# Weight units one unit later in the load queue, and the sample stage laid out anew, in a two-layer hybrid decoder step

## The chip, the cores and the metric

The kernel runs on one core of a Trainium2 chip, as one launch. The metric is the device time of an execution in microseconds. Before the change it is 2910.22 us, the median of three runs (2906.68 to 2913.82). The profile is that of one further execution, which took 2911.25 us; its span, from the first to the last instruction, is 2909.6 us.

## The reference

One inference step of two layers for a prompt of 256 tokens and for a sample group of 8 sequences of 8 new tokens behind 1024 past ones: 320 token columns, which share all weights. Model width 2048, MLP width 8192, all in f32.

```
layer 0   z = rmsnorm(x) @ w_in                   # rx rg | q kc vc ks vs kw vw | gates
          A) rx -> causal conv (4) -> RG-LRU scan;  y_rnn = gelu(rg) * h       (1024 channels)
          B) sparse attention, 16 query heads, 4 kv heads of 64, three branches:
             compressed  blocks of 64 tokens -> k, v by a small MLP (w1, gelu, w2)
             selected    prompt: all its blocks; sample: 16 blocks, chosen by the compressed probabilities
             window      the last 512 tokens
             o = sum of branches * sigmoid gates
          x += concat(y_rnn, o) @ w_out ;  x += relu(rmsnorm(x) @ ff1)^2 @ ff2
layer 1   x += gated short convolution (w_in, w_out) ;  x += the same MLP
```

A sample reads its past keys and values through a page table: 8 pages of 128 rows for the compressed branch, 8 for the selected one, and 512 window rows. The outputs also hold the new keys, values, windows and recurrent states.

## The kernel before

**Weights.** Every large product runs in `gemm` (L173). A weight unit is 512 KB; `w_dma` (L133) loads it on SP's queue into one of four buffers (`NRAW`). ScalarE and VectorE split it into two numbers of the matmul type, a high part `whi` (`S.copy`, L145) and the rest `wlo` (L146), in six half units (`NSP`). Each weight tile then gives three matmuls of 320 columns (L204 to L206), 24 in a unit. `w_fill` (L149) runs before each half unit: it issues the conversions up to three units ahead of the matmuls, and then the loads:

```
while st["dma"] < min(st["conv"] // 2 + NRAW, len(units)):
    w_dma()
```

**Slots.** After each unit `side()` counts a slot and issues what `at(n, f)` has put there, in the order of the calls. All other work of layer 0 is hung into slots in this way. Each engine takes its instructions in program order; so a wait holds all that stands behind it on the same engine. DMAs issued by `SP` and `G` stand in the order of those queues too. Slots 1 to 42 are the projections of keys, values, queries and gates, 43 to 74 those of rx and rg, in eight groups of four slots (`C0 = 42`); then comes the first half of the output projection, 16 units.

**Compression** (slots 5 to 46). `cmp_load` brings eight pages of a sequence on SP (eight register reads of page numbers, then eight DMAs, tile `cx`), `cmp_swap` (L703) turns them into `cy` by two copies on VectorE, one on POOL, one on ScalarE, and `cmp_mm` (L713) multiplies by `w1`, which `cmp_load_w` (L679) has loaded on SP. Right behind the matmuls the two halves of their sum are emptied, for 16 pages in two rounds of a copy on ScalarE (L719) and an add on VectorE (L720) into `hid`, a part of `yr`.

**Prompt stage** (slots 45 to 63, `P3 = 45`). `pr_slot` (`pr_scores`, `pr_softmax`, `pr_scale`, `pr_trans`, `pr_pv`) takes one head pair and branch per slot. The recurrence of rx runs beside it: per pair of channel chunks `rec_conv`, `rec_gates`, three steps of `rec_scan` (the scan itself is L616, in `rec_scan_c`), `rg_gelu_a`, `rg_gelu_b` and `rec_y` (L625, POOL). For the last pair these are slots 70 to 76.

**Sample stage** (from slot 65, `P4 = 65`, three slots per sequence). `sa_open` (L1182, slot 63) opens its buffers in memory that the prompt stage has left, loads the first keys and hangs in the sixteen copies that lay out the queries (`sa_q`, L1201, POOL) and the first value loads (`sa_load_v`, L1160, on POOL's queue, with eight register reads per sequence). `sa_begin` (slot 64) makes the first keys' scores: queries by compressed keys and by the new keys, the first softmax; `sa_select` (slot 66) chooses the blocks. Per sequence b: `sa_kt` in slots n, n and n+1 turns the three key tiles `kl` (L1168) and then loads the next sequence's on SP (L1153); `sa_scores` (L1264) and `sa_softmax` (L1288 to L1296) in n+2; `sa_trans` (L1307) in n+4; `sa_pv` (L1325 to L1330) in n+5, which at its end issues the value loads of the next sequence; `sa_ot` (L1341) in n+7. PSUM has three banks for `gemm`, four `a` for all small work and one `o`.

**Between the stages.** After the last rg unit two `side()` run without weight matmuls, the memory of the recurrence and of `yh`, `yl` is given back, `xh`, `xl` and `y` are made there, `y` is loaded from DRAM on ScalarE's queue (L1422), eight chunks of `yr` are split (L445, L446), a third `side()` runs, and the output projection begins; `half_evac` (L1432) adds its sums to `y`.

Of the kernel before, what the change touches and what calls it, by code (L numbers as in the profile page):

```python
# [11 lines left out]
F32 = mybir.dt.float32  # L12
# [58 lines left out]
def tile_hybrid_step(ctx: ExitStack, tc: tile.TileContext, A, O, stop=None, dbg=None):  # L71
# [181 lines left out]
    kc_x = kb.tile([128, 4, 8], F32, name="kc_x")  # L253
    vc_p = kb.tile([64, 8, 2, 64], F32, name="vc_p")
    kt = {b: kb.tile([128, 2, N], F32, name="kt_" + b) for b in ("s", "w")}
    kx = {b: kb.tile([128, 2, NP_TOK], F32, name="kx_" + b) for b in ("s", "w")}
    vp = {b: kb.tile([128, 2, 256], F32, name="vp_" + b) for b in ("s", "w")}
    gp = kb.tile([128, 2, 48], F32, name="gp")
    tbc = kb.tile([128, 2, 4, 16], F32, name="tbc")
# [446 lines left out]
    def cmp_mm(bp, i, pages):  # L706

        y = cx.pop(("y", bp, i)).rearrange("p d h s n -> p d (h s n)")
        p = bank("a")
        n = pages * 8  # L710
        for d in range(16):
            for u in range(2):
                PE.matmul(p[64 * u:64 * u + 64, :n], w1[:, i, 16 * u + d], y[:, 16 * u + d],  # L713
                          start=d == 0, stop=d == 15)
        nh = min(pages, 8)
        for k in range(pages // nh):
            h = hid[64 * i:64 * i + 64, 16 * bp + 8 * k:16 * bp + 8 * k + nh].rearrange("p n g s -> p s (n g)")
            q = p[:, 64 * k:64 * k + 8 * nh].rearrange("p (s n) -> p s n", s=2)
            S.copy(h, q[64 - 64 * i:128 - 64 * i])  # L719
            V.tensor_tensor(h, q[64 * i:64 * i + 64], h, ALU.add)  # L720
# [281 lines left out]

    p3x = ctx.enter_context(ExitStack())
    p3 = tb = pct_p = None

    def p3_open():
        nonlocal p3, tb, pct_p
        cmpx.close()
        ev.close()
        p3 = p3x.enter_context(pool("p3", "right"))  # L1010
# [125 lines left out]
    p4 = ld = None  # L1136
# [9 lines left out]
    def sa_load_k(b, c):  # L1146
        k = ld.tile([128, 4, 256], F32, name="kl", bufs=3)
# [27 lines left out]
    def sa_open():  # L1175
        nonlocal ld, p4, pc, pcT, snew, mnew, badd, wtab, ot_s, qx
        ld = p4x.enter_context(pool("ld", "right"))
        p4 = p4x.enter_context(pool("p4", "right"))
        pc = p4.tile([128, NB, 16], F32, name="pc")
        pcT = p4.tile([128, 128], F32, name="pcT")  # L1180
        snew = p4.tile([128, 2, NB, NT], F32, name="snew")
        mnew = p4.tile([128, 2, NB], F32, name="mnew")  # L1182
        badd = p4.tile([128, NB, 16], F32, name="badd")
        wtab = p4.tile([128, 512], F32, name="wtab")
        ot_s = p4.tile([128, 8, NB * NT], F32, name="ot_s")
# [19 lines left out]
    def sa_begin():  # L1205
        V.tensor_copy(wtab[:, :384], near[:, 0:1].to_broadcast([128, 384]))
# [22 lines left out]
        mx = p4.tile([128, NB], F32, name="mx")  # L1229
# [7 lines left out]
    def sa_select():  # L1237
        mx = p4.tile([128, NB], F32, name="mx")
# [6 lines left out]
        im = p4.tile([128, NB, 14], F32, name="im")  # L1245
# [21 lines left out]
    def sa_softmax(b):  # L1267
# [26 lines left out]
        V.tensor_tensor(l[:, 0:2], l[:, 0:2], l[:, 2:4], ALU.add)  # L1294
        V.reciprocal(l[:, 0:2], l[:, 0:2])
        V.tensor_tensor(l[:, 0:2], l[:, 0:2], gs[:, 1:3, b], ALU.mult)  # L1296
        sj["p", b] = (s, l)

    def sa_trans(b):
        s, l = sj["p", b]  # L1300
        t = p4.tile([128, 14, 128], F32, name="pT")
        sj["pt", b] = t
        for i in range(4):
            p = bank("a")
            n = min(4, 13 - 4 * i)
# [29 lines left out]
    def sa_ot(b):  # L1335
        r = sj.pop(("o", b))
        o = bank("a")
# [31 lines left out]
    def p3_close():  # L1369
        p3x.close()  # L1370
        kbx.close()
# [17 lines left out]
    P4 = P3 + 20  # L1389
    at(P4 - 1, sa_begin)  # L1390
    at(P4 + 1, sa_select)
# [19 lines left out]
    for _ in range(2):  # L1411
        side()
    rgp.close()
    base.close()
    actp = ctx.enter_context(ExitStack())
    act = actp.enter_context(pool("act"))

    xh = act.tile([128, 16, N], F32R, name="xh")
    xl = act.tile([128, 16, N], F32R, name="xl")
# [14 lines left out]
    run(gemm(8, 8, lambda k: (xh[:, k], xl[:, k]), half_evac, 256))  # L1434
# [10 lines left out]
    p4x.close()  # L1445
    l0.close()
# [245 lines left out]
```

## Time and profile before

| of the profiled execution | |
|---|---|
| time / span | 2911.25 / 2909.6 us |
| TensorE (PE) busy | 2846.3 us, 98% |
| VectorE (DVE) busy | 1618.6 us, 56% |
| ScalarE (ACT) busy | 1213.1 us, 42% |
| GpSimd (POOL) busy | 378.2 us, 13% |
| moved by DMA | 463.98 MB, 159 GB/s as a mean |
| mean granted TensorE clock | 0.990 |

The page gives the busy time of each engine; the answers of the trace give waits (who waited for whom), windows (busy time, granted clock and DMA share in a stretch), instructions of a line, and a timeline. In a timeline a row is start, duration, engine, line, operation, what it writes and reads, how many were merged, and in brackets the idle time of the engine before it with what ended it. The DMA share is the mean busy share of the core's 16 DMA engines.

### The profile page before, as it was taken

The page shows a single profiled execution, that of the slowest core. Times are in us where ns is not written, and L with a number is a line of the kernel's source. Part 1 is how long each engine was busy: PE and PEld are TensorE (multiplying, and loading weights), DVE is VectorE, ACT ScalarE, POOL GpSimd, SP SyncE. Part 2 cuts the span into 40 slices and gives each one's busy share as a digit, 9 for nine tenths or more (in the row PEclk, how much of TensorE's full clock was granted, in tenths as well). Part 3 has the DMA queues.
Part 4 walks back from the last instruction along what each step waited for, and adds up shares of the span by engine and source line. Part 5 has one row for each costly group of instructions (what it writes and reads, how often), then busy time and mean ns, then how long its engine had stood idle before and what let it go on. Part 6 is the DMA issues. An engine that isn't in the chain of part 4 may idle for free.

```text
span 2909.6 us, 53661 instructions
## 1 busy us (share of the span) xinstructions
PE 2846.3 (98%) x20947; PEld 2785.6 (96%) x20947; DVE 1618.6 (56%) x2937; ACT 1213.1 (42%) x2336; POOL 378.2 (13%) x555
## 2 busy tenths in 40 slices
PE   8999987999999999999999999999999999999999
PEld 7998776899999999999999999999999999999999
DVE  6796677774444544544465555555444444544544
ACT  4555644354334434434443333344433433433433
POOL 2323353230010010010010111111011011001000
PEclk9999989999999999999999999999999999999999
DMA  8765258645445555555445444444444444544543
GB/s 244 213 198 156 73 147 257 210 138 162 165 154 167 165 159 161 165 166 153 153 144 156 152 147 150 147 153 148 149 152 145 153 152 149 149 152 148 149 157 119
DMA packets 275997, 463.98 MB, mean 159 GB/s; under 512 B 19050, under 2 KB 100694, under 8 KB 275215
## 3 DMA queue, kind: packets, MB, share of 16 engines
q1 hardware_dynamic: 268254, 438.47, 49.1%
q0 software_dynamic: 6864, 19.44, 2.1%
q8 instruction: 164, 2.69, 0.4%
q10 hardware_dynamic: 624, 2.64, 0.2%
q14 instruction: 91, 0.74, 0.1%
HBM read 452.95 MB, written 15.92 MB: 161 GB/s over the span
## 4 chain that ended last, share of the span: by engine, by line
PE 81%; DVE 0%; DMA 0%; ACT 0%; issue 0%; DVEq 0%; ACTq 0%
PE ps_g L204 27%; PE ps_g L206 27%; PE ps_g L205 27%; DMA wraw<-in_w_out_e_dram 0%; PE ps_a L1652 0%; DVE wlo L146 0%; PE ps_a L1264 0%; PE ps_o L1325 0%; PE ps_a L1307 0%; DVE ktl L1168 0%; PE ps_a L633 0%; PE ps_a L1624 0%; DVE rs L1473 0%; PE ps_a L436 0%; DVE y L1475 0%
## 5 line engine op out<-in xcount | busy, mean ns | idle before, releaser
L146 DVE TENSOR_TENSOR wlo<-wraw,whi 128x512 fp32r<-128x512 f32 x1488 | 1007.4, 718 | 1122.3 <-ACT whi L145 1121.5
L145 ACT CAST whi<-wraw 128x512 fp32r<-128x512 f32 x1492 | 854.1, 617 | 1377.8 <-PE ps_g L206 1334.0
L204 PE MATMUL ps_g<-yl,whi 128*128 128x320 f32 x3408 | 1066.9, 313 | 10.9 <-DVE kv L817 5.1
L205 PE MATMUL ps_g<-yh,wlo 128*128 128x320 f32 x3408 | 1056.8, 310 | 0.0
L206 PE MATMUL ps_g<-yh,whi 128*128 128x320 f32 x3408 | 1056.6, 310 | 0.0
L204 PE MATMUL ps_g<-xl,whi 128*128 128x320 f32 x2560 | 796.2, 311 | 11.3 <-DVE xl L446 7.3
L206 PE MATMUL ps_g<-xh,whi 128*128 128x320 f32 x2560 | 792.7, 310 | 0.0
L205 PE MATMUL ps_g<-xh,wlo 128*128 128x320 f32 x2560 | 792.7, 310 | 0.0
L204 PEld LDWEIGHTS ps_g<-yl,whi 128*128 128x128 f32 x3408 | 643.2, 189 | 22.3 <-issue 8.4
L205 PEld LDWEIGHTS ps_g<-yh,wlo 128*128 128x128 f32 x3408 | 643.3, 189 | 1.7 <-issue 0.2
L206 PEld LDWEIGHTS ps_g<-yh,whi 128*128 128x128 f32 x3408 | 643.2, 189 | 0.0
L204 PEld LDWEIGHTS ps_g<-xl,whi 128*128 128x128 f32 x2560 | 482.4, 188 | 13.1 <-DVE xl L446 7.7
L205 PEld LDWEIGHTS ps_g<-xh,wlo 128*128 128x128 f32 x2560 | 482.4, 188 | 0.0
L206 PEld LDWEIGHTS ps_g<-xh,whi 128*128 128x128 f32 x2560 | 482.1, 188 | 0.0
L1477 POOL TENSOR_TENSOR y<-y,rs 128x320 f32<-128x320 f32 x96 | 92.3, 994 | 1257.8 <-DVE rs L1473 1257.8
L1473 DVE TENSOR_TENSOR rs<-ps_g,r 128x320 f32<-128x320 f32 x128 | 60.6, 488 | 25.1 <-PE ps_g L206 25.0
L1506 DVE TENSOR_TENSOR fr<-fr 128x320 f32<-128x320 f32 x128 | 62.3, 487 | 11.1 <-ACT xh L1509 11.1
L431 POOL TENSOR_TENSOR nacc<-nacc,nsq 128x320 f32<-128x320 f32 x45 | 44.1, 980 | 172.0 <-ACT nsq L427 170.4
L1507 DVE TENSOR_TENSOR xl<-fr,xh 128x320 fp32r<-128x320 f32 x128 | 62.9, 492 | 4.4
L1509 ACT ACTIVATE xh<-fr 128x320 fp32r<-128x320 f32 x128 | 60.3, 471 | 4.1
L1503 ACT ACTIVATE fr<-ps_g 128x320 f32<-128x320 f32 x128 | 56.1, 438 | 5.7 <-PE ps_g L206 5.7
L1586 POOL TENSOR_TENSOR xx<-cg,r 128x256 f32<-128x256 f32 x16 | 13.1, 819 | 278.4 <-DVE xx L1584 278.4
(382 smaller groups left out, 1426.3 us busy)
## 6 DMA issues: line engine op xcount, KB each, us to landing
wraw<-in_w_ff_dram SPq DMA_DIRECT2D x512, 512.0 KB, 3.7
wraw<-in_w_in_o_dram SPq DMA_DIRECT2D x96, 512.0 KB, 3.7
wraw<-in_w_in_e_dram SPq DMA_DIRECT2D x74, 512.0 KB, 5.3
wraw<-in_w_out_e_dram SPq DMA_DIRECT2D x32, 512.0 KB, 5.5
wraw<-in_w_out_o_dram SPq DMA_DIRECT2D x32, 512.0 KB, 3.9
cx<-in_cache_cmp_k_dram SPq DMA_DIRECT2D x64, 128.0 KB, 2.1
cx<-in_cache_cmp_v_dram SPq DMA_DIRECT2D x64, 128.0 KB, 3.4
kl<-in_cache_sel_k_dram SPq DMA_DIRECT2D x64, 128.0 KB, 3.6
```

What stands on the lines that cost most here:

```text
L145: S.copy(h, r)
L146: (G if u < 4 and hf == 0 else V).tensor_tensor(l, r, h.bitcast(F32), ALU.subtract)
L204: PE.matmul(ps[m][:, :N], wh, al, start=k + j == 0, stop=False)
L205: PE.matmul(ps[m][:, :N], wl, ah, start=False, stop=False)
L206: PE.matmul(ps[m][:, :N], wh, ah, start=False, stop=k + j == nk - 1)
L431: G.tensor_tensor(nacc["t"], nacc["t"], sq, ALU.add)
L1473: V.tensor_tensor(t, ps[:, :N], scale, ALU.mult)
L1477: after(1, lambda: G.tensor_tensor(y[:, c], y[:, c], t, ALU.add))
L1503: S.activation(t, ps[:, :N], AF.Relu)
L1506: V.tensor_tensor(t, t, t, ALU.mult)
L1507: V.tensor_tensor(xl[:, c], t, xh[:, c].bitcast(F32), ALU.subtract)
L1509: after(1, lambda: S.activation(xh[:, c], t, AF.Square))
```

## The change

- Weight loads: `w_fill` keeps one unit less issued ahead of the conversions, so a unit stands one place later in SP's queue. The buffers are the same four.
- `cmp_load_w` issues its loads on POOL (`G`).
- The compression sum is emptied by `cmp_evac`, hung into the next slot (the last one at once), with one copy and one add for all pages.
- The prompt's keys, values and gates (pool `keep_b`) become views of one tile `kba`; in the sample stage the value tiles and `ot_s` lie in it.
- A new pool `ldk`, opened with the prompt stage, holds the key tiles and the small tables. `sa_begin` moves to slot 50, `sa_select` to 52, the first key loads to 55, 56 and 57; `P4` is 64. The first value loads move one slot forward, to between the query copies; four of the sixteen query copies go to ScalarE.
- The scaling factors `l` move from `sa_softmax` to `sa_trans`. `sa_ot` takes bank `o`.
- The first half of the output projection uses `yh`, `yl` as `xh`, `xl`: six chunks are split right after the last rg unit, the first projection unit runs, then one `side()` without weight matmuls, the `y` loads and the split of the last two chunks.

```diff
-        while st["dma"] < min(st["conv"] // 2 + NRAW, len(units)):
+        while st["dma"] < min(st["conv"] // 2 + NRAW - 1, len(units)):
...
+    kba = kb.tile([128, 4608], F32, name="kba")
...
-            SP.dma_start(w1[64 * hf:64 * hf + 64, i], A["cmp_w1_" + nm_][0][:, 32 * hf:32 * hf + 32])
-        SP.dma_start(w2[64 * i:64 * i + 64, 64 * i:64 * i + 64], A["cmp_w2_" + nm_][0])
+            G.dma_start(w1[64 * hf:64 * hf + 64, i], A["cmp_w1_" + nm_][0][:, 32 * hf:32 * hf + 32])
+        G.dma_start(w2[64 * i:64 * i + 64, 64 * i:64 * i + 64], A["cmp_w2_" + nm_][0])
...
+        if (bp, i) == (3, 1):
+            cmp_evac(bp, i, pages, p)
+        else:
+            at(st["slot"] + 1, cmp_evac, bp, i, pages, p)
+
+    def cmp_evac(bp, i, pages, p):
         nh = min(pages, 8)
-        for k in range(pages // nh):
...
+        h = hid[64 * i:64 * i + 64, 16 * bp:16 * bp + pages].rearrange("p (k n) g s -> p k s (n g)", n=nh)
+        q = p[:, :8 * pages].rearrange("p (k s n) -> p k s n", k=pages // nh, s=2)
+        S.copy(h, q[64 - 64 * i:128 - 64 * i])
+        V.tensor_tensor(h, q[64 * i:64 * i + 64], h, ALU.add)
...
-        v = ld.tile([128, 4, 256], F32, name="vl", bufs=4)
+        o = 1024 * ((3 * b + c) % 4)
+        v = kba[:, o:o + 1024].rearrange("p (n c) -> p n c", n=4)
...
-        for c in range(3):
-            sa_load_k(0, c)
...
-            at(n + 2, sa_load_v, 0, c)
-        at(n + 4, sa_load_v, 1, 0)
+            at(n + 1, sa_load_v, 0, c)
+        at(n + 3, sa_load_v, 1, 0)
...
-                G.tensor_copy(
+                (G.tensor_copy if gg or half else S.copy)(
...
-        o = bank("a")
+        o = bank("o")
...
-    P4 = P3 + 20
-    at(P4 - 1, sa_begin)
-    at(P4 + 1, sa_select)
+    P4 = P3 + 19
+    at(P3 + 5, sa_begin)
+    at(P3 + 7, sa_select)
+    for c in range(3):
+        at(P3 + 10 + c, sa_load_k, 0, c)
...
-    for _ in range(2):
-        side()
+
+    xh, xl = yh, yl
+    for c in range(0, 6, 2):
+        split(xh[:, c:c + 2], xl[:, c:c + 2], yr[:, c:c + 2])
+    half = gemm(8, 8, lambda k: (xh[:, k], xl[:, k]), lambda g, m, ps: half_evac(g, m, ps), 256)
+    next(half)
+    side()
     rgp.close()
-    base.close()
...
     for c in range(4):
         S.dma_start(y[:, 4 * c:4 * c + 4], xt_d[:, 4 * c:4 * c + 4])
-    for c in range(0, 8, 2):
-        split(xh[:, c:c + 2], xl[:, c:c + 2], yr[:, c:c + 2])
-    side()
+    split(xh[:, 6:8], xl[:, 6:8], yr[:, 6:8])
...
-    run(gemm(8, 8, lambda k: (xh[:, k], xl[:, k]), half_evac, 256))
+    run(half)
```

## Rows read from the trace of the kernel before

**Rows 1.** Windows: stretch, busy us of each engine (instructions), clock, DMA share, GB/s.

```profile
600.00:2905.00 2305.00, 2304.43 (x15724) 2302.37 (x15722) 1172.27 (x1966) 908.80 (x1695) 180.08 (x243) 1.00 0.49 153
```

**Rows 2.** Waits of TensorE, 60 to 240 us: total us, times, longest us.

```profile
PE ps_g L204 <- DVE kv L817: 5.1, 2, 4.2
PE ps_a L713 <- DMA w<-in_cmp_w_k_dram: 4.1, 1, 4.1
PE ps_g L204 <- DVE qr L882: 4.0, 2, 2.9
PE ps_a L713 <- DVE yr L703: 2.5, 1, 2.5
```

**Rows 3.** Windows as in rows 1: length; PE, PEld, DVE, ACT, POOL; clock; DMA.

```profile
60.00:120.00 60.00, 52.50 (x490) 50.07 (x489) 39.81 (x48) 28.45 (x43) 19.58 (x17) 0.89 0.81 221
120.00:240.00 120.00, 111.74 (x955) 107.22 (x954) 103.04 (x133) 61.67 (x94) 27.60 (x19) 0.97 0.64 188
285.00:390.00 105.00, 100.52 (x685) 81.00 (x684) 70.40 (x230) 66.86 (x184) 43.85 (x83) 0.97 0.26 76
390.00:430.00 40.00, 34.33 (x327) 30.83 (x326) 32.21 (x73) 20.10 (x38) 24.21 (x34) 0.87 0.69 199
```

**Rows 4.** Timeline around 50 to 61 us: POOL's first compression copy, SP's compression weight.

```profile
51.79 2.04 POOL L703 COPY cy<-cx 64x1024 f32<-64x1024 f32 x1 [0.36 <-issue]
...
60.19 1.16 SPq L679 DMA_DIRECT2D w<-in_cmp_w_k_dram  x2
```

**Rows 5.** Waits of ScalarE and of SP's queue, 60 to 240 us.

```profile
ACT yr L719 <- PE ps_a L713: 36.1, 9, 5.8
ACT yr L719 <- DVE yr L720: 12.4, 8, 5.6
...
SPq L133 <- DVE wlo L146: 30.3, 14, 6.0
```

**Rows 6.** Waits of TensorE, 380 to 590 us.

```profile
PE ps_g L204 <- DVE y L1432: 4.1, 3, 2.0
PE ps_a L1307 <- DVE pT L1308: 1.7, 1, 1.7
...
PE ps_a L1341 <- DVE or L1330: 1.3, 1, 1.3
```

**Rows 7.** Instructions of three lines on POOL: count, ns min/median/max, first and last start.

```profile
L1201 POOL COPY qx<-qbd x16: 599/791/1112, 386.9 to 399.4; 32x512 f32<-32x512 f32 x16
...
L1160 POOL DMA_DIRECT2D vl<-in_cache_sel_v_dram x64: 537/537/612, 401.8 to 559.3; - x64
...
L625 POOL TENSOR_TENSOR yr<-ii,yr x4: 1547/1560/1591, 321.2 to 479.0; 128x640 f32<-128x640 f32 x4
```

**Rows 8.** Timeline of the sample stage: first scores, POOL's loads, the stretch without weights.

```profile
419.79 2.97 PE L1264 MATMUL ps_a<-ktl,qx 32*32 32x384 f32 x50 [5.67 <-DVE ktl L1168]
...
461.63 2.29 POOL L1160 DMA_DIRECT2D vl<-in_cache_sel_v_dram  x4 [5.96 <-PE ps_o L1325]
...
468.48 0.88 DVE L522 TENSOR_TENSOR yr<-ps_g,rt 128x320 f32<-128x320 f32 x2
...
469.21 2.29 POOL L1160 DMA_DIRECT2D vl<-in_cache_sel_v_dram  x4 [4.53 <-PE ps_a L1307]
...
475.60 1.22 DVE L1168 STREAM_TRANSPOSE ktl<-kl 128x1024 f32<-128x1024 f32 x1
...
483.98 0.35 ACTq L1422 DMA_DIRECT2D y<-xt_d  x1
...
487.94 0.64 PE L204 MATMUL ps_g<-xl,whi 128*128 128x320 f32 x1 [5.61 <-DVE xl L446]
...
499.74 1.92 PE L1264 MATMUL ps_a<-ktl,qx 32*32 32x384 f32 x64
```

**Rows 9.** Waits of VectorE and of SP's queue, 380 to 590 us.

```profile
DVE l L1294 <- ACT sp L1292: 12.6, 8, 1.6
...
SPq L133 <- DVE wlo L146: 90.3, 20, 8.1
```

More of the change, by code (lines that the diff above doesn't have):

```diff
@@ L252, in tile_hybrid_step, with kview @@
     kb = kbx.enter_context(pool("keep_b", "right"))
[L253 to L259, printed above, removed]
+    kba = kb.tile([128, 4608], F32, name="kba")
+    ko = [0]
+    def kview(parts, *dims):
+        n = math.prod(dims)
+        v = kba[:parts, ko[0]:ko[0] + n]
+        ko[0] += n
+        names = "abc"[:len(dims)]
+        return v.rearrange(f"p ({' '.join(names)}) -> p {' '.join(names)}", **dict(zip(names, dims)))
+    kc_x = kview(128, 4, 8)
+    vc_p = kview(64, 8, 2, 64)
+    kt = {b: kview(128, 2, N) for b in ("s", "w")}
+    kx = {b: kview(128, 2, NP_TOK) for b in ("s", "w")}
+    vp = {b: kview(128, 2, 256) for b in ("s", "w")}
+    gp = kview(128, 2, 48)
+    tbc = kview(128, 2, 4, 16)
     evp = ev.enter_context(pool("evp", "right"))
@@ L714, in cmp_mm @@
                           start=d == 0, stop=d == 15)
-        nh = min(pages, 8)
-        for k in range(pages // nh):
[L717 to L720, printed above, removed]
+        if (bp, i) == (3, 1):
[3 more added lines that the diff above has]
+    def cmp_evac(bp, i, pages, p):
+        nh = min(pages, 8)
+        h = hid[64 * i:64 * i + 64, 16 * bp:16 * bp + pages].rearrange("p (k n) g s -> p k s (n g)", n=nh)
+        q = p[:, :8 * pages].rearrange("p (k s n) -> p k s n", k=pages // nh, s=2)
+        S.copy(h, q[64 - 64 * i:128 - 64 * i])
+        V.tensor_tensor(h, q[64 * i:64 * i + 64], h, ALU.add)
     def cmp_gelu():
@@ L1000, in tile_hybrid_step @@
         return
+    lkx = ctx.enter_context(ExitStack())
+    ldk = None
     p3x = ctx.enter_context(ExitStack())
@@ L1006, in p3_open @@
     def p3_open():
-        nonlocal p3, tb, pct_p
+        nonlocal p3, tb, pct_p, ldk
         cmpx.close()
         ev.close()
+        ldk = lkx.enter_context(pool("ldk", "right"))
         p3 = p3x.enter_context(pool("p3", "right"))
@@ L1135, in tile_hybrid_step @@
     p4x = ctx.enter_context(ExitStack())
-    p4 = ld = None
+    p4 = None
     SEL = [A["cache_sel_k"][0].rearrange("n s g d -> n s (g d)"),
@@ L1146, in sa_load_k @@
     def sa_load_k(b, c):
-        k = ld.tile([128, 4, 256], F32, name="kl", bufs=3)
+        k = ldk.tile([128, 4, 256], F32, name="kl", bufs=3)
         sj["k", b, c] = k
@@ L1175, in sa_open @@
     def sa_open():
-        nonlocal ld, p4, pc, pcT, snew, mnew, badd, wtab, ot_s, qx
-        ld = p4x.enter_context(pool("ld", "right"))
+        nonlocal p4, ot_s, qx
         p4 = p4x.enter_context(pool("p4", "right"))
[L1179 to L1185, printed above, removed]
+        ot_s = kba[:, 4096:].rearrange("p (c t) -> p c t", c=8)
         qx = p4.tile([128, 2, NB, 128], F32, name="qx")
-        for c in range(3):
-            sa_load_k(0, c)
         n = st["slot"]
@@ L1205, in sa_begin @@
     def sa_begin():
+        nonlocal pc, pcT, snew, mnew, badd, wtab
+        pc = ldk.tile([128, NB, 16], F32, name="pc")
+        pcT = ldk.tile([128, 128], F32, name="pcT")
+        snew = ldk.tile([128, 2, NB, NT], F32, name="snew")
+        mnew = ldk.tile([128, 2, NB], F32, name="mnew")
+        badd = ldk.tile([128, NB, 16], F32, name="badd")
+        wtab = ldk.tile([128, 512], F32, name="wtab")
         V.tensor_copy(wtab[:, :384], near[:, 0:1].to_broadcast([128, 384]))
@@ L1227, in sa_begin @@
         V.tensor_reduce(mnew.rearrange("p r b -> p (r b)"), sn, AX.X, ALU.min)
-        mx = p4.tile([128, NB], F32, name="mx")
+        mx = ldk.tile([128, NB], F32, name="mx")
         V.tensor_reduce(mx, pc, AX.X, ALU.max)
@@ L1237, in sa_select @@
     def sa_select():
-        mx = p4.tile([128, NB], F32, name="mx")
+        mx = ldk.tile([128, NB], F32, name="mx")
         p = bank("a")
@@ L1244, in sa_select @@
         V.tensor_copy(pcT, p[:, 128:256])
-        im = p4.tile([128, NB, 14], F32, name="im")
+        im = ldk.tile([128, NB, 14], F32, name="im")
         V.tensor_copy(im, p[:, :128].rearrange("p (b k) -> p b k", k=16)[:, :, 1:15])
@@ L1293, in sa_softmax @@
                          bias=nm[:, 2 + br:3 + br], scale=-1.0, accum_out=l[:, 2 + br:3 + br])
-        V.tensor_tensor(l[:, 0:2], l[:, 0:2], l[:, 2:4], ALU.add)
-        V.reciprocal(l[:, 0:2], l[:, 0:2])
-        V.tensor_tensor(l[:, 0:2], l[:, 0:2], gs[:, 1:3, b], ALU.mult)
         sj["p", b] = (s, l)
@@ L1309, in sa_trans @@
                 t[:, 4 * i:4 * i + n].rearrange("p c k -> p (c k)"), p[:, :128 * n])
+        V.tensor_tensor(l[:, 0:2], l[:, 0:2], l[:, 2:4], ALU.add)
+        V.reciprocal(l[:, 0:2], l[:, 0:2])
+        V.tensor_tensor(l[:, 0:2], l[:, 0:2], gs[:, 1:3, b], ALU.mult)
         G.tensor_scalar(t[:, 13], pcT, cm[:, C_BM + b:C_BM + b + 1], 1.0, op0=ALU.mult, op1=ALU.mult)
@@ L1370, in p3_close @@
         p3x.close()
-        kbx.close()
         sa_open()
@@ L1410, in tile_hybrid_step @@
     run(gemm(8, 16, yact, rx_or_rg, 256))
-    for _ in range(2):
-        side()
-    rgp.close()
-    base.close()
[L1415 to L1419, printed above, removed]
+    xh, xl = yh, yl
[4 more added lines that the diff above has]
+    side()
+    rgp.close()
     y = ctx.enter_context(pool("ypl")).tile([128, 16, N], F32, name="y")
@@ L1445, in tile_hybrid_step @@
     p4x.close()
+    lkx.close()
+    kbx.close()
     l0.close()
```

## The prediction, made before the changed kernel ran

> **What bounds the kernel now.** I read the windows first. From 600 us to the end TensorE is busy without a hole at a granted clock of 1.00: 15724 matmuls in 2305 us, 147 ns each, so a weight unit (24 matmuls) takes 3.5 us [rows 1]. Nothing there can be shortened by an order of work, and on SP that stage holds hardly anything but weights, which wait for the same conversions wherever they stand in the queue: I cost the new order at nothing there. Everything to be won lies in the first 600 us. Second, what TensorE waited for: 15.7 us between 60 and 240 us [rows 2], and between 380 and 590 us pieces of 5.7 and 5.6 us [rows 8] and of 4.1, 1.7 and 1.3 us [rows 6]. Third, the clock: after such holes the granted clock is 0.89 over 60 to 120 us, 0.97 over 120 to 240, 0.87 over 390 to 430 [rows 3]; what is missing to 1.00 is time at the lower level (1.2 instead of 2.4 GHz) and costs 0.11 x 60 = 6.6 us, 3.6 us and 5.2 us. Then I went to the queue behind each hole.
>
> **The sum against the profiled execution** (2911.25 us, span 2909.6; 1.0 above the median of the three runs shown).
>
> *1. The first compression weight goes from SP to POOL: -7.4.* SP issues it at 60.19 us [rows 4], and TensorE stands 4.1 us until it has landed [rows 2]. It comes so late because SP stood before: from 60 to 240 us weight units wait 30.3 us on SP for a conversion, with everything behind them [rows 5]. In POOL's order its issue stands ahead of the first compression copy, which runs at 51.79 [rows 4]; a megabyte that starts 8 us earlier, for a wait of 4.1, is there in time. I count the 4.1 us and half of the 6.6 us of slow clock. Bounds: 0 (it lands no earlier) and -7.4. The three issues cost POOL 0.5 to 0.7 us each, as on SP; the copy that waits behind them is needed only when TensorE gets to the 4.1 us hole.
>
> The Trainium skill speaks against this step (SBUF — State Buffer, "SBUF: two separate sides"): a DMA from the GpSimd queue has its descriptors written by GpSimd, and VectorE copies can lock it out, so that the transfer seems blocked. By that rule the weight would come no earlier and this term be 0. The trace shows 64 POOL issues of 0.54 to 0.61 us in the busiest VectorE stretch, which look unblocked beside VectorE's work of that stage [rows 7]. It is kept as a rival.
>
> *2. Compression loads pass one weight unit: -2.5.* The second hole (2.5 us, VectorE's copy of the position encodings, loaded by SP at the end of the same jam [rows 2]) has the other half of the slow clock: 5.8 us in all. The loads now stand behind one weight unit less. But TensorE also arrives earlier, by term 1, and the engines stay loaded. I take less than half. Bounds 0 and -5.8.
>
> *3. The compression sums are emptied one slot later, in one copy and one add instead of two and two: -8.* ScalarE waits for the compression matmuls 36.1 us in nine places and another 12.4 us for VectorE between the two halves [rows 5]; its casts stand behind, VectorE's subtractions behind those, and then TensorE finds no free sum: 5.1 + 4.0 us of waits [rows 2], and 3.6 us of slow clock [rows 3]: 12.7 us. All of it can't come back: VectorE is busy 103.0 of these 120 us [rows 3], 96% of the 107 that would be left. I take two thirds; the last compression (emptied at once as before) keeps its wait, which is off the path. Bounds -3 and -12.7. The sum stays in its bank a slot longer; in those slots no other operation takes one.
>
> *4. First keys and block choice move into the prompt stage: +1.* The same matmuls run there, so TensorE's work is equal. VectorE gets 22 small instructions, under 10 us by the 0.44 us that one lasts on average where they stand now (73 in 32.2 us, 390 to 430); from 285 to 390 us it is busy 70.4 of 105 us [rows 3], so they fit, though in a slot that also holds a scan. Bounds 0 and +4. The key loads of the first sample move to the same stage, where the DMA share is 0.26: nothing.
>
> *5. Start of the sample stage: -6.3.* The 5.7 us wait for the transposed keys [rows 8] goes: the choice no longer stands before the third transpose, and the keys have long landed. Half of the 5.2 us of slow clock goes with it; the other half followed the small matmuls and moves with them. What is late next is POOL: twelve of the sixteen query copies stay there, at about 0.85 us from 386.9 on [rows 7], and now the first value loads stand before the last three: 386.9 + 9 x 0.85 + 10 (eight register reads, 4.5 [rows 8], and nine issues of 0.54 [rows 7]) + 3 x 0.85 = 407.1. The first scores ran at 419.8 [rows 8]; without the wait (5.7), one weight unit (3.5) and the moved matmuls with their slow clock (by estimate 5), TensorE is there between 405 and 406. I add 2. Bounds -8.3 and 0.
>
> *6. Sample slots: -3.0.* The bank wait of the transposes (1.7) goes, since the output turn takes another bank; the 1.3 us wait for the output sum goes, since the sums' scaling factors are made a slot later [rows 6]. Bounds 0 and -4.
>
> *7. The stretch without weight matmuls: +3.2.* This is where I expect a loss. Now VectorE begins to empty the last gate group at 468.48, and TensorE gets weight matmuls again at 487.94; the second unit is done at 499.74 [rows 8]: 31.3 us. After the change, from the same point: to the end of the third key transpose 8.3 us, less 2.4 for two such transposes (1.22 each) that lie a slot earlier, plus some 1.3 for the factors and the split: the first unit starts at 7.2. It takes 5 (3.5 at full clock, more after a hole), the scores 2 (their 64 matmuls last 1.92 [rows 8]), the values as much; these start at 14.2. Now POOL: the value loads of the next sample stand in slot 75, the last gate product (`rec_y(3)`, 1.56 us [rows 7]) in slot 76. Until now it stood before them. One group of loads takes 469.21 + 2.29 - 461.63 = 9.9 us [rows 8], starting about 1 us after the values: the product is ready at 26.7 (14.2 + 1 + 9.9 + 1.6). Behind it wait the y loads and the split of the last two chunks, as now from 483.98 to 487.94, 4.0 us [rows 8]: 30.7. The rest of the second unit (1.8) and the transposes that were done before it until now (some 2) give 34.5, against 31.3. If POOL didn't hold it, 14.2 + 2 + 3.5 + 2 = 21.7: a gain of 9.6. Bounds -9.6 and +8 (slow clock throughout).
>
> *8. Second half of the output projection: -3.5.* VectorE waits eight times, 12.6 us, for ScalarE's exponentials before it makes the factors [rows 9], and y is added after that, so TensorE waits 4.1 us for sums [rows 6]. The factors now wait in the next slot. Bounds 0 and -5.
>
> Sum: -7.4 - 2.5 - 8 + 1 - 6.3 - 3.0 + 3.2 - 3.5 = -26.5; 2911.25 - 26.5 = 2884.8. I say **2885 us**, about 0.9% faster.
>
> **The rivals.**
> *A. POOL does not hold the last gate product* (term 7 at its lower end). For it: the loads wait for buffers, and if these are free earlier the group starts earlier. Against: the order is fixed, and reads and issues alone are 9.9 us. 12.8 us less: 2872.
> *B. The early holes form again.* VectorE at 96% and a DMA share of 0.81 as a mean over 60 us speak for it [rows 3]; against it, ScalarE's 48.5 us of waits are real time in a queue that feeds VectorE [rows 5]. With 5 of the 17.9 us of terms 1 to 3: 2898.
> *C. The compression weight lands late from POOL* (the skill's rule above), a mechanism of this kernel with term 1 at 0: 2892.
> *D. Slower: weights starve in the sample stage.* Each weight unit now stands behind one more group of key loads, which themselves wait for transposes: eight register reads and twelve issues per sample, some 10 us of SP by POOL's like group [rows 8]. It decides when that exceeds the time SP has to spare: today it waits 90.3 us in twenty places for conversions before weights, 13 us per sample, so weights were issued as soon as a buffer came free, and the group fits [rows 9]. If the transposes ran late enough to eat it, I price 5 us in each of seven samples: 2885 + 35 = 2920.
>
> **How the numbers follow.** Forecast 0.51, its own range 2875 to 2895; A 0.15; B 0.22; C 0.06; D 0.06. The range from 2864 to 2902 holds the forecast, A, C and most of B. Faster or slower by over 0.3% (8.7 us, about what a measurement of this kernel can tell from no change) is below 2901.5 or above 2919: faster 0.51 + 0.15 + 0.06 + 0.14 of B = 0.86; same 0.08 of B and 0.01 of D; slower 0.05.
>
> **What would show it.** Right: no TensorE wait for the compression weight, whose issue stands on POOL before 56 us; ScalarE's longest waits at the compression copies gone; first scores within 2 us after their weight unit; VectorE's wait before the factors gone; and one hole of some 10 us between the first and second unit of the output projection, with POOL in value loads and `rec_y(3)` behind them. From 600 us on (shifted) nothing but 147 ns per matmul. Wrong: new TensorE waits for sums between 120 and 240 us as long as now (B), waits of TensorE for the conversion of a weight that has just landed (D), or no hole in the projection (A).

## The result: slower by half a per cent, and the profile after

The changed kernel takes 2923.66 us (median of 5 runs, 2920.69 to 2925.42) against 2906.68 us of the kernel before beside it: ratio 1.0054, 95% interval 1.0042 to 1.0067, some 16 us slower. I had forecast 2885, with 0.86 on faster. The profiled execution took 2923.66 us, span 2922.0.

Windows of the changed kernel: stretch, length, busy us of PE, PEld, DVE, ACT and POOL (instructions), granted clock, DMA share, GB/s.

```profile
612.00:2917.00 2305.00, 2304.67 (x15724) 2302.56 (x15723) 1171.97 (x1966) 909.29 (x1697) 180.48 (x243) 1.00 0.49 153
60.00:120.00 60.00, 48.50 (x485) 46.33 (x484) 32.80 (x45) 26.25 (x39) 18.83 (x20) 0.91 0.75 207
120.00:240.00 120.00, 107.96 (x900) 103.18 (x900) 100.78 (x126) 59.08 (x83) 26.04 (x17) 0.97 0.66 197
...
480.00:540.00 60.00, 41.69 (x724) 36.30 (x728) 37.42 (x84) 20.16 (x47) 19.27 (x31) 0.80 0.72 207
```

The long stage is what it was, 15724 matmuls in 2305 us [rows 1]. From 60 to 240 us TensorE is busy 7.8 us less than before (156.5 against 164.2 [rows 3]). The clock is hardly better there (0.91 and 0.97, against 0.89 and 0.97), and from 480 to 540 us it is 0.80.

Waits from 60 to 240 us in the changed kernel, first TensorE's, then ScalarE's, then SP's: total us, times, longest.

```profile
PE ps_g L204 <- DVE kv L833: 12.8, 3, 8.8
PE ps_g L204 <- DVE qr L898: 6.2, 3, 2.6
PE ps_a L847 <- ACT hsq L842: 2.6, 1, 2.6
PE ps_a L724 <- ACT tok L824: 1.9, 1, 1.9
...
ACT whi L145 <- DMA wraw<-in_w_in_e_dram: 55.0, 11, 12.0
...
SPq L696 <- DVE cy L714: 37.0, 7, 12.4
SPq L133 <- DVE wlo L146: 19.4, 7, 7.3
```

Two of the waits that I meant to remove are gone: TensorE has none for the compression weight, and ScalarE has no line at the compression sums, where [rows 5] had 36.1 and 12.4 us. But TensorE's waits for sums, which the second of these was to remove, have grown, and the four lines of TensorE sum to 23.5 us against 15.7 [rows 2], and ScalarE now waits 55.0 us for weights to land. On SP the loads of compression pages wait for buffers (37.0 us), with the weight units behind them. The timeline of the worst of these holes (start, us, engine, operation, idle before and its releaser):

```profile
71.41 4.35 SPq L696 DMA_DIRECT2D cx<-in_cache_cmp_v_dram  x8
75.82 0.57 SPq L133 DMA_DIRECT2D wraw<-in_w_in_e_dram  x1
...
86.96 0.62 ACT L145 CAST whi<-wraw 128x512 fp32r<-128x512 f32 x1 [12.01 <-DMA wraw<-in_w_in_e_dram]
...
87.61 0.69 DVE L146 TENSOR_TENSOR wlo<-wraw,whi 128x512 fp32r<-128x512 f32 x1 [11.86 <-ACT whi L145]
88.22 0.88 DVE L833 TENSOR_TENSOR kv<-ps_g,rt 128x320 f32<-128x320 f32 x2
...
88.76 0.64 PE L204 MATMUL ps_g<-yl,whi 128*128 128x320 f32 x1 [8.79 <-DVE kv L833]
```

Read it from below: TensorE waits for a sum that VectorE has to empty; VectorE stands 11.9 us in its subtraction, for a cast; ScalarE stands 12.0 us in that cast, for a weight that SP issued behind eight page loads. TensorE's wait is shown as one for a sum; its cause is two engines further back.

In the sample stage and the output projection TensorE waits as follows (380 to 600 us):

```profile
PE ps_g L204 <- DVE yl L457: 23.0, 3, 12.8
PE ps_a L1282 <- DVE ktl L1188: 9.7, 4, 7.1
PE ps_g L204 <- DVE y L1448: 1.7, 2, 1.2
PE ps_a L1322 <- ACT sp L1307: 1.5, 1, 1.5
```

The two longest have their own timelines. At 433 us (the 7.1), VectorE and POOL beside it:

```profile
430.06 1.29 DVE L146 TENSOR_TENSOR wlo<-wraw,whi 128x512 fp32r<-128x512 f32 x2 [3.39 <-ACT whi L145]
433.56 3.97 DVE L146 TENSOR_TENSOR wlo<-wraw,whi 128x512 fp32r<-128x512 f32 x2
...
433.51 1.53 POOL L547 TENSOR_TENSOR yr<-yr,aa 128x640 f32<-128x640 f32 x1
435.12 1.86 POOL L636 TENSOR_TENSOR yr<-ii,yr 128x640 f32<-128x640 f32 x1
...
440.60 0.95 PE L1282 MATMUL ps_a<-ktl,qx 32*32 32x384 f32 x16 [7.15 <-DVE ktl L1188]
```

A pair of such subtractions lasts 1.29 us without POOL's products beside it, and the next pair 3.97 with them; the third key transpose, for which TensorE waits, is queued behind. And between the first and second unit of the output projection (the 12.8):

```profile
475.67 0.48 DVE L533 TENSOR_TENSOR yr<-ps_g,rt 128x320 f32<-128x320 f32 x1
...
484.64 0.64 PE L204 MATMUL ps_g<-yl,whi 128*128 128x320 f32 x1 [8.46 <-DVE yl L457]
...
492.77 0.43 PE L1343 MATMUL ps_o<-kba,pT 128*32 128x64 f32 x16
...
493.43 2.47 POOL L1180 DMA_DIRECT2D kba<-in_cache_sel_v_dram  x4
...
501.52 2.48 POOL L1180 DMA_DIRECT2D kba<-in_cache_sel_v_dram  x4 [4.55 <-issue]
504.01 1.54 POOL L636 TENSOR_TENSOR yr<-ii,yr 128x640 f32<-128x640 f32 x1
...
509.42 0.64 PE L204 MATMUL ps_g<-yl,whi 128*128 128x320 f32 x1 [12.81 <-DVE yl L457]
```

POOL works off the value loads before the last gate product (L636), as term 7 of the prediction said.

### The profile page after: what moved, and what is told of

It reads as the page before. It is cut to its first block, busy times and chain, and to the rows that moved or that the text cites. A ratio compares the mean times of both kernels' runs of the same rounds, so it can differ in the third digit from the quotient of the medians.

```text
span 2922.0 us, 53642 instructions
## 1 busy us (share of the span) xinstructions
PE 2844.1 (97%) x20947; PEld 2784.6 (95%) x20947; DVE 1608.1 (55%) x2929; ACT 1213.4 (42%) x2332; POOL 374.6 (13%) x557
## 4 chain that ended last, share of the span: by engine, by line
PE 81%; DVE 0%; ACT 0%; issue 0%; DMA 0%; ACTq 0%; SPq 0%; DVEq 0%; POOL 0%
PE ps_g L204 27%; PE ps_g L205 27%; PE ps_g L206 27%; PE ps_a L1282 0%; PE ps_o L1343 0%; PE ps_a L1322 0%; PE ps_a L1670 0%; DMA kl<-in_cache_win_k_dram 0%; DVE sp L1306 0%; DVE ktl L1188 0%; ACT sp L1307 0%; ACT yh L456 0%; ACT sp L1308 0%; PE ps_o L1359 0%; ACT sp L1310 0%
## 5 line engine op out<-in xcount | busy, mean ns | idle before, releaser
L204 PE MATMUL ps_g<-yl,whi 128*128 128x320 f32 x5968 | 1865.0, 312 | 44.2 <-DVE yl L457 23.0
L206 PE MATMUL ps_g<-yh,whi 128*128 128x320 f32 x5968 | 1851.7, 310 | 0.0
L205 PE MATMUL ps_g<-yh,wlo 128*128 128x320 f32 x5968 | 1851.7, 310 | 0.0
L204 PEld LDWEIGHTS ps_g<-yl,whi 128*128 128x128 f32 x5968 | 1127.4, 189 | 55.9 <-DVE yl L457 23.7
L205 PEld LDWEIGHTS ps_g<-yh,wlo 128*128 128x128 f32 x5968 | 1127.5, 189 | 1.6 <-issue 0.2
L206 PEld LDWEIGHTS ps_g<-yh,whi 128*128 128x128 f32 x5968 | 1127.3, 189 | 0.0
L1525 DVE TENSOR_TENSOR yl<-fr,yh 128x320 fp32r<-128x320 f32 x128 | 62.9, 492 | 4.4
L1527 ACT ACTIVATE yh<-fr 128x320 fp32r<-128x320 f32 x128 | 60.4, 472 | 4.0
L1503 DVE SCALAR_TENSOR_TENSOR yl<-y,par,yh 128x320 fp32r<-128x320 f32 x48 | 43.0, 921 | 0.0
L714 DVE COPY cy<-cx 64x1024 f32<-64x1024 f32 x32 | 35.4, 1105 | 0.2
```

The costliest lines, as they stand in the source:

```text
L204: PE.matmul(ps[m][:, :N], wh, al, start=k + j == 0, stop=False)
L205: PE.matmul(ps[m][:, :N], wl, ah, start=False, stop=False)
L206: PE.matmul(ps[m][:, :N], wh, ah, start=False, stop=k + j == nk - 1)
L714: (V.tensor_copy, G.tensor_copy, V.tensor_copy, S.copy)[k](y[64 * half:64 * half + 64, :, s_], v[64 * s_:64 * s_ + 64, :, half].rearrange( ...
L1525: V.tensor_tensor(xl[:, c], t, xh[:, c].bitcast(F32), ALU.subtract)
L1527: after(1, lambda: S.activation(xh[:, c], t, AF.Square))
```

## The experiments

Every ratio is to the kernel before, run beside it on the same chip, with its 95% interval; 0.0010 is 2.9 us. Differences between kernels are taken from these ratios. Base is the changed kernel unless said otherwise.

**The order of the weight units, and the last gate product.** Four kernels; in each diff the line taken out is that of the base.

a_order:
```
-        while st["dma"] < min(st["conv"] // 2 + NRAW - 1, len(units)):
+        while st["dma"] < min(st["conv"] // 2 + NRAW, len(units)):
```


> The changed kernel with weight units issued at the old place in the queue of loads (NRAW units ahead of the conversion instead of NRAW - 1); all else as changed. Theory N (the order starves the weights: ScalarE waits 57.9 us in 13 places for a weight load to land, against 6.8 us in one place before, and VectorE's and ScalarE's queues stand behind it): ScalarE's waits for weight loads fall under 15 us, the TensorE hole of 8.8 us at 80 us falls under 3, and the time falls by 8 to 14 us to 2910 to 2916. Rival E (the early loss comes from the late emptying of the compression sums or from the loads on POOL): the hole stays, time 2920 to 2925.

b_order is the kernel before with the same line the other way round (`NRAW` to `NRAW - 1`).

> The kernel before with that one edit alone (NRAW - 1). Theory N: it is slower than before by 6 to 14 us, 2913 to 2921, and ScalarE's waits for weight loads rise from 6.8 to over 30 us. Rival E: 2904 to 2909.

a_recy:
```
-        at(n + 10, rec_y, pr)
+        at(n + (9 if pr == 3 else 10), rec_y, pr)
```


> The changed kernel with the last gate product (rec_y of the last pair) one slot earlier, so that on POOL it stands ahead of the value loads of a slot later. Theory Y (POOL holds the product behind two groups of value loads, and TensorE waits 12.8 us for the split that needs it): the hole between the first and second unit of the output projection falls under 4 us, with less slow clock after it, and the time falls by 8 to 13 us to 2911 to 2916. Rival (the split waits for something else in that stretch, the y loads or VectorE's transposes): hole over 8 us, time over 2919.

a_order_recy has both edits.

> Both edits on the changed kernel. If the two losses are separate, they add: 2898 to 2906, at or under the kernel before. If what one gives back is lost again at the other (TensorE comes earlier to the same late load), it is within 4 us of the better of the two single ones.

Measured: a_order 1.0025 (1.0016 to 1.0034), 8.4 us faster than the change; b_order 1.0034 (1.0022 to 1.0047), 9.9 us slower than before; a_recy 1.0020 (1.0011 to 1.0029), 9.9 us faster than the change; a_order_recy 1.0002 (0.9993 to 1.0011), 15 us faster. ScalarE's waits for weights, 60 to 240 us, in a_order:

```profile
ACT whi L145 <- DMA wraw<-in_w_in_e_dram: 12.0, 3, 7.8
```

and in b_order:

```profile
ACT whi L145 <- DMA wraw<-in_w_in_e_dram: 31.2, 9, 6.3
```

Theory N holds from both sides: the order alone costs 8 to 10 us. Where it costs them can be read from VectorE's first addition for the attention gates, late in the early stage. In the kernel before and in b_order:

```profile
L902 DVE TENSOR_TENSOR gt<-ps_g,rt x1: 427/427/427, 207.7 to 207.7; 64x256 f32<-64x256 f32 x1
L902 DVE TENSOR_TENSOR gt<-ps_g,rt x1: 428/428/428, 214.0 to 214.0; 64x256 f32<-64x256 f32 x1
```

In the four kernels here that have the new order it starts at 212.9 to 216.0 us, in the sixteen with the old one at 199.9 to 210.0. In the changed kernel ScalarE has no wait for a weight's load from 240 to 612 us, so the sample stage has no part in this loss.

In a_recy POOL runs the product at once, and TensorE's wait between the first and the second unit falls from 12.8 to 3.6 us, so Y holds too:

```profile
474.47 0.88 DVE L533 TENSOR_TENSOR yr<-ps_g,rt 128x320 f32<-128x320 f32 x2
...
491.58 1.10 PE L1343 MATMUL ps_o<-kba,pT 128*32 128x64 f32 x64
...
492.25 1.57 POOL L636 TENSOR_TENSOR yr<-ii,yr 128x640 f32<-128x640 f32 x1
...
493.89 2.20 POOL L1180 DMA_DIRECT2D kba<-in_cache_sel_v_dram  x4
...
497.35 0.72 ACT L456 CAST yh<-yr 128x640 fp32r<-128x640 f32 x1 [0.70 <-issue]
...
499.06 0.42 PE L204 MATMUL ps_g<-yl,whi 128*128 128x320 f32 x1 [3.64 <-DVE yl L457]
...
502.72 1.66 PE L1322 MATMUL ps_a<-cm,sp 128*128 128x128 f32 x13
```

Singly the two edits give 18.3 us and together 15; the kernel with both is outside the 2898 to 2906 that I had expected of separate losses, but the intervals leave room for a full sum. They explain the loss, but not where the 27 us went that the other terms were to bring: with both out of the way the kernel is level with the one before.

**Undoing what I had priced highest.** On a_order:

a_order_wsp (term 1 undone):
```
-            G.dma_start(w1[64 * hf:64 * hf + 64, i], A["cmp_w1_" + nm_]...)
+            SP.dma_start(w1[64 * hf:64 * hf + 64, i], A["cmp_w1_" + nm_]...)
-        G.dma_start(w2[64 * i:64 * i + 64, 64 * i:64 * i + 64], ...)
+        SP.dma_start(w2[64 * i:64 * i + 64, 64 * i:64 * i + 64], ...)
```


> The changed kernel with the weight units at their old place (as in a_order, 2915.2) and the compression weights issued by SP again, as before the change. If term 1 holds (the issue on POOL takes away the wait for the first compression weight, 4.1 us and the slow clock behind it): slower than a_order by 4 to 7 us, 2919 to 2922, with a TensorE wait for that weight at 68 us. If the weight would be early enough in any queue, or the jam on SP only moves: 2913 to 2917.

a_order_evac0 (term 3 undone: the two copies and two additions stand in `cmp_mm` again):
```
-            at(st["slot"] + 1, cmp_evac, bp, i, pages, p)
+        for k in range(pages // nh):
...
+            S.copy(h, q[64 - 64 * i:128 - 64 * i])
+            V.tensor_tensor(h, q[64 * i:64 * i + 64], h, ALU.add)
```


> The same base with the compression sums emptied at once and in two copies and two additions, as before the change. If term 3 holds with two thirds of its size: slower than a_order by 6 to 10 us, 2921 to 2925, with ScalarE waiting over 30 us for the compression matmuls. If the time that ScalarE waits there is hidden: 2913 to 2917 although those waits are back.

a_order_wsp_evac0 undoes both.

> The changed kernel with the weight units at their old place (a_order, 2915.2) and both other edits of the early stage undone: compression weights issued by SP, sums emptied at once in two halves. Undone singly, neither cost anything (2914.1 and 2915.1). Theory D (the stretch from 60 to 85 us is bound by the transfers, whose share there is 9 tenths or more in all slices; a load taken forward pushes another back): again 2912 to 2917. Rival (each of the two covers for the other, and together they carry the gain that I forecast): 2922 to 2930.

Measured: 1.0023 (1.0014 to 1.0032), 1.0024 (1.0014 to 1.0035) and 1.0018 (1.0009 to 1.0027), against 1.0025 of a_order. Neither term brings anything that can be told from nothing, singly or together, although in a_order_evac0 ScalarE's waits are back:

```profile
ACT yr L730 <- PE ps_a L724: 33.3, 8, 5.3
ACT yr L730 <- DVE yr L731: 16.8, 8, 5.3
ACT yr L714 <- DMA tok<-in_cmp_pe_k_dram: 7.0, 1, 7.0
```

The third line is a small load that ScalarE waits for with and without term 3 (5.4 us in a_order).

**The sample stage.** On a_order_recy:

c_p4late:
```
-    P4 = P3 + 19
+    P4 = P3 + 20
```


> The changed kernel with both edits (a_order_recy, 2909.8) and every step of the sample stage one slot later, at the slots of the kernel before. Theory S: with the earlier slot the first transposes of the probabilities fall beside POOL's products of the gates (VectorE's two subtractions at 433 us last 3.97 us instead of 1.25) and TensorE waits 7.1 us for keys; a slot later the hole is under 3 us and the time falls by 3 to 7 us to 2903 to 2907. Rival: the hole is VectorE's own work of that slot and comes back a slot later, or what it gives goes to the start of the stage: 2908 to 2913.

c_begin_late, on c_p4late:
```
-    at(P3 + 5, sa_begin)
-    at(P3 + 7, sa_select)
+    at(P4 - 1, sa_begin)
+    at(P4 + 1, sa_select)
```


> The kernel c_p4late (2910.9) with the first keys' scores and the choice of blocks put back out of the prompt stage to where they stood before, just ahead of the sample stage's first steps. If terms 4 and 5 hold (the choice no longer stands before the third transpose: -6.3, +1): slower than c_p4late by 3 to 7 us, 2914 to 2918, with a TensorE wait of 4 to 6 us for keys at the first scores. If what is gained there is lost again to the next wait of the stage: 2909 to 2913.

c_split (the first three splits at the head of the last gate slot):
```
-    run(gemm(8, 16, yact, rx_or_rg, 256))
...
+    gates = gemm(8, 16, yact, rx_or_rg, 256)
+    for _ in range(31):
+        next(gates)
+    for c in (4, 2, 0):
+        later.setdefault(st["slot"] + 1, deque()).appendleft(
+            (split, (xh[:, c:c + 2], xl[:, c:c + 2], yr[:, c:c + 2])))
+    run(gates)
```


> The same base with the split of the first six chunks for the output projection put ahead of the side work of the last gate slot (scan, transposed probabilities, factors) instead of behind it. Theory O: TensorE waits 8.5 us there because VectorE and ScalarE come to the split only after that side work: the hole falls under 4 us, and of the 5 us some come back as a wait for keys right after the first unit: time lower by 2 to 5 us, 2905 to 2908. Rival: all of it comes back (2909 to 2911).

d_gelu, on c_split:
```
-        at(n + 9, rg_gelu_b, pr)
-        at(n + (9 if pr == 3 else 10), rec_y, pr)
+        at(n + (12 if pr == 2 else 9), rg_gelu_b, pr)
+        at(n + (12 if pr == 2 else 9 if pr == 3 else 10), rec_y, pr)
```


> The kernel c_split (2907.1) with the last step of the gate function and the gate product of pair 2 some slots later, away from the slot in which VectorE subtracts, copies probabilities and transposes keys. Theory P (POOL's products beside them stretch VectorE's two subtractions from 1.25 to 3.95 us): they last 1.25 to 1.4 us again, the TensorE wait for keys at 427 to 433 us falls from 5.9 to 3.5 or less, time 2903 to 2905. Rival (the slot is bound by VectorE's order): subtractions and hole stay, 2906 to 2909.

Measured: c_p4late 1.0012 (1.0003 to 1.0021), S fails, and its rival holds: the keys' wait falls from 7.1 to 4.6 us, and one of 4.9 us for a gate sum stands before the first scores instead. c_begin_late 1.0008 (0.9999 to 1.0017): the wait at the first scores is back (5.5 us), that at the second ones is gone, and the time is that of c_p4late. c_split 0.9998 (0.9989 to 1.0007), 1.2 us less than a_order_recy by the ratios, which can't be told from nothing: the wait before the first unit falls from 8.5 to 1.5 us, as O says, but TensorE's waits for keys from 380 to 600 us rise from 9.8 to 16.8 us, so that in waits nearly all of it comes back, as the rival says. d_gelu 1.0004 (0.9995 to 1.0013), no gain, but its trace bears on P. VectorE at the old place and at the new one, then the new wait of TensorE:

```profile
426.14 1.25 DVE L146 TENSOR_TENSOR wlo<-wraw,whi 128x512 fp32r<-128x512 f32 x2
...
445.40 2.78 DVE L146 TENSOR_TENSOR wlo<-wraw,whi 128x512 fp32r<-128x512 f32 x2
...
450.18 0.33 PE L1322 MATMUL ps_a<-cm,sp 128*128 128x128 f32 x1 [3.77 <-ACT ii L595]
```

P's mechanism is right: without POOL's products beside them the subtractions last 1.25 us (2.59 in c_split) and the keys' wait falls from 5.9 to 4.4. Its size is not: P had put that wait at 3.5 us or less, so most of it is VectorE's order of work. The products stretch VectorE's work where they stand now (2.78 us), and TensorE has a new wait of 3.8 us near them; that they cause it is not shown. The move brought no time.

**The small load behind the weights.** In c_split TensorE's longest wait before 240 us is 5.8 us for position encodings, which SP issues at 81.41 us. d_pe, on c_split:
```
-            SP.dma_start(x[0:64, 2], A["cmp_pe_" + "kv"[i]][0]...)
+            G.dma_start(x[0:64, 2], A["cmp_pe_" + "kv"[i]][0]...)
```


> The kernel c_split (2907.1) with the two small loads of the position encodings (64 KB each) issued by POOL, ahead of its compression copies, instead of SP, where they wait behind weight units (81.41 us; TensorE waits 5.8 us for them in the end). Theory Q (they are late because of their queue): that hole falls under 2 us, 2902 to 2905. Theory D (transfers bound this stretch): the hole moves to another wait between 65 and 95 us, 2906 to 2909.

Measured: 0.9978 (0.9969 to 0.9987), 2901.12 us: 6.4 us faster than the kernel before, the first version with a gain. The load and the wait in c_split:

```profile
81.41 0.53 SPq L703 DMA_DIRECT2D tok<-in_cmp_pe_k_dram  x1
...
87.21 0.31 PE L724 MATMUL ps_a<-yr,w 128*64 128x24 f32 x2 [5.79 <-DVE yr L714]
```

and in d_pe:

```profile
70.41 0.52 POOL L703 DMA_DIRECT2D tok<-in_cmp_pe_k_dram  x1
...
82.98 0.24 PE L724 MATMUL ps_a<-yr,w 128*64 128x24 f32 x2 [1.40 <-DVE yr L714]
```

Q holds, and D falls: 64 KB could be had 11 us earlier, and no other wait of TensorE from 60 to 240 us grew by more than 0.1 us. That raised the question whether this load had hidden terms 1 and 3. On d_pe: e_pe_old13 undoes both terms, f_pe_wsp the first alone, f_pe_evac0 the third alone (edits as in a_order_wsp and a_order_evac0); e_pe_ord has `NRAW - 1` again; e_pe_fact makes the factors in `sa_softmax` again instead of `sa_trans`; e_b_pe is the kernel before with d_pe's edit alone.

> The kernel d_pe (2901.1: position encodings loaded from POOL) with terms 1 and 3 undone (compression weights from SP, sums emptied at once in two halves). Theory L (the late small load ended the early stage and hid whatever was won ahead of it): with it early the two terms show, 5 to 12 us slower, 2906 to 2913. Rival W (the stage is bound by VectorE's work and by the transfers): 2899 to 2904.

> The kernel d_pe (2901.1) with the compression weights issued by SP again, as before the change. If term 1 carries the 7 us (wait for that weight back at 68 to 72 us): 2905 to 2909. If term 3 does: 2900 to 2903. If they share it: 2903 to 2906.

> The kernel d_pe with the compression sums emptied at once in two halves again. If term 3 carries the 7 us (ScalarE's waits for the compression matmuls hold its casts): 2905 to 2909. If term 1 does: 2900 to 2903. If they share it: 2903 to 2906.

> The kernel d_pe with the weight units issued one unit later again, as in the change. Theory N (weights starve behind the compression loads by themselves): still 6 to 12 us slower, 2907 to 2913, and ScalarE's waits for weight loads over 40 us. Rival (the order cost only by pushing the small loads or by the crowd around them): 2899 to 2905.

> The kernel d_pe with the factors of the sums made right behind the exponentials again, as before the change. If terms 6 and 8 hold for this part: 3 to 5 us slower, 2904 to 2906, with TensorE waits of 4 us for y in the second half of the projection. If VectorE's wait is hidden: 2900 to 2903.

> The kernel before with that one edit alone (the two loads of the position encodings on POOL). Theory L, if the compression weight on SP is the earlier wait there: the 2.5 us hole goes, the 4.1 us one stays, 2 to 4 us faster, 2903 to 2906. If the small load was the whole of it: 6 us faster, 2900 to 2903. If it is hidden before: 2906 to 2909.

Measured, with the difference to d_pe:

| kernel | ratio | interval | to d_pe |
|---|---|---|---|
| e_pe_old13 | 1.0002 | 0.9992 to 1.0011 | +7.0 us |
| f_pe_wsp | 0.9993 | 0.9984 to 1.0002 | +4.4 |
| f_pe_evac0 | 0.9984 | 0.9975 to 0.9993 | +1.7 |
| e_pe_ord | 0.9999 | 0.9990 to 1.0008 | +6.1 |
| e_pe_fact | 0.9983 | 0.9974 to 0.9992 | +1.5 |
| e_b_pe | 0.9993 | 0.9984 to 1.0003 | (2.0 us below the kernel before) |

With the load early, terms 1 and 3 together are worth 7 us, where they were worth nothing before: theory L. Term 1 seems to carry more of it: in f_pe_wsp TensorE waits 3.7 us for that weight, while in f_pe_evac0 its waits for sums are 9.4 us against 9.3 in d_pe. But the intervals of both kernels overlap d_pe's, so the shares stay open. The order costs 6 us here too, with ScalarE's waits for weights at 46.0 us in eleven places. The factors' 1.5 us, and the 2.0 us that the small load's move gives alone on the kernel before, can't be told from nothing. In e_b_pe the load is issued at 70.42 us instead of 79.72, and the 2.5 us hole of [rows 2] that I had expected to go is still there:

```profile
PE ps_a L713 <- DVE yr L703: 2.5, 1, 2.5
```

So the load alone did not make that hole: in the kernel before VectorE works without a pause from 79.50 us until its copies of the encodings end at 89.00.

## Why the prediction was wrong, by its steps

**Term 2 had the wrong sign, and is the first half of the loss** (-2.5 forecast, bounds 0 and -5.8; measured +8.4 and +9.9, with d_pe +6.1). I looked at which loads get past a weight unit and not at what the unit then stands behind. My rival D has just this mechanism, but I put it in the sample stage, where SP waits 90.3 us [rows 9], and left it out of the early stage, where SP has 30.3 us [rows 5] against groups of eight page loads that wait for VectorE's copies. The bound at zero had no reason behind it. The gain that I set against it was misread as well: the 2.5 us hole stays when the load comes 9 us earlier (e_b_pe).

**Term 7 was right in kind; its size was about 5 us short.** From the first evacuation of the last gate group (475.67) I had put the first unit at 7.2 us, the values at 14.2, the product at 26.7 and the second unit's continuation at 30.7. Measured from the rows above: 484.64, that is 9.0; 492.77, 17.1; 504.01 + 1.54, 29.9; 509.42, 33.8. POOL's group took what I had worked out (12.8 from the values to the product, 12.5 forecast), and the 3 us came before it: 1.8 before the first unit, where two small operations on the factors last 0.56 and 1.40 us beside POOL's work (L540, L541), against 0.15 and 0.16 at 516 us, and 1.1 between the first unit and the values. Transposes included, the stretch ends at 515.4 us, 39.7 long, against 34.5 forecast and 31.3 before; the clock from 480 to 540 us is 0.80. The hole is the second half of the loss: a_recy gives 9.9 us back.

In the kernel before, TensorE waited twice in this stretch, 5.6 us [rows 8] and, longer than any wait that I had listed, 7.1:

```profile
476.51 0.45 PE L1307 MATMUL ps_a<-cm,sp 128*128 128x128 f32 x1 [7.12 <-ACT ot_s L1342]
```

In the changed kernel the two waits are 8.5 and 12.8 us, in a_recy 8.3 and 3.6, hardly less than before. So the term's lower end, which is rival A's price, was off by more. In a_recy POOL does not hold the product, and the stretch, from 474.47 to the end of the transposes at 504.38, is 29.9 us long: 1.4 less than before, where I had 9.6 less. I had let the second unit go on 2 us after the values begin; it goes on 7.5 us after them, since its split stands on ScalarE behind the exponentials and the y loads until 497.35.

**Terms 1 and 3** (-7.4, -8): undone on a_order, neither costs anything that can be told from nothing. In term 1 the wait for the weight went as forecast, and I took it as time that would come back by itself. What came next was the position encodings: with the weight early they are the next wait in line, 4.5 us in a_order. Term 3 failed one link earlier. I had let ScalarE's waits at the compression hold its casts, these VectorE's subtractions, and these TensorE's sums. Those waits of ScalarE are gone in d_pe, too, and TensorE waits 9.3 us for sums there, against 9.1 in [rows 2]:

```profile
PE ps_g L204 <- DVE kv L833: 4.9, 3, 3.5
PE ps_g L204 <- DVE qr L898: 4.4, 3, 3.3
...
ACT whi L145 <- PE ps_g L206: 33.9, 15, 5.7
```

ScalarE now waits 33.9 us for TensorE's matmuls before its next casts, against 6.6 us before: its waits at the compression were slack and not on TensorE's path. With the encodings early the two terms give 7.0 of my 15.4. What still holds the sums is open: VectorE's 100.8 of 120 us in that stage would fit, but no run shows it as the cause.

**Terms 4 and 5** (+1, -6.3) were undone only together: that costs nothing (c_begin_late against c_p4late), so they bring nothing. The wait at the first scores fell to 1.9 and 0.6 us, and the second scores got one of 7.1, which [rows 6] does not have: the stage was no longer held back by its start, and is held in its next slot, by VectorE's order of work and in part by POOL's products (d_gelu). **Terms 6 and 8** (-3.0, -3.5): the bank wait and the output turn's wait went, one of 1.5 us for exponentials came; the waits for y fell from 4.1 [rows 6] to 1.7. In time the factors' place gives 1.5 us, which can't be told from nothing.

The two losses are 15 us together and the kernel without them is level (a_order_recy). There all my other terms, with term 7 at its lower end of -9.6, should have given 37 us, of which 8 are that lower end's own error. So the larger error is not the missed loss but a sum of gains: waits, each with its own row, added as if nothing else were nearly as late. Of the rivals D (0.06) has the nearest number, 2920, and that is luck: it is 35 us of loss in the sample stage on top of 26 us of gains, where there were 15 us of loss and no gains. B, with 0.22, describes what became of the early gains (holes form again), at 2898; A is refuted. C is not seen: the weight issued by POOL leaves no TensorE wait at all. That does not test the rule of the Trainium skill that speaks for C in the prediction (SBUF — State Buffer, "SBUF: two separate sides"): the changed kernel issues that weight from 53.49 to 55.06 us, and VectorE's next copy starts at 59.03.

VectorE's stretched subtractions answer to another sentence of the Trainium skill (SBUF — State Buffer, "SBUF: two separate sides"): VectorE and GpSimd share one pair of ports, and when a VectorE instruction with two inputs in SBUF meets a GpSimd one that reads SBUF, whichever starts first has the pair to its end while the other stands. The trace agrees: 3.97 us beside two of POOL's products, 1.29 without them. The prediction cites the same section for DMA issues and passes this one by, although it moved VectorE's work against POOL's by a slot.

## What to carry to other kernels

A wait that a profile shows is not yet time that its removal brings; before adding two of them up, look for the load or result that comes next at the same place, and move that one too. Where a wait on one engine is said to hold another, check that each link of the chain is late: ScalarE's 48.5 us here held nothing that the time shows. Where a queue serves two kinds of loads, cost a new order for both: what moves forward, and what then stands behind a group that waits for buffers. And read a TensorE wait for a sum backwards through the queues of VectorE and ScalarE: here the cause of one was a weight's load, two engines back.

## What the runs showed of the hardware

Two of POOL's products on SBUF (1.53 and 1.86 us) beside two of VectorE's subtractions stretch these from 1.29 to 3.97 us, and moving the products by some slots moves the stretching (2.78 us), with no gain in time. Two 64 KB loads moved to another queue, the first of them issued 11 us earlier, were worth 6 us, in a stretch where the DMA engines are busy throughout: for each 5 us from 65 to 85 us the windows give a share of 0.95 to 1.08, in c_split and d_pe alike. I had read a high share as a limit; here the order in which the loads were issued was worth time all the same.
